# Strided attention on one core: another order of the first loads, stores of two groups at once, and transposes ahead of the sums

## The chip, the cores and the metric

The kernel runs on one core of a Trainium2 chip. The metric is the device time of one execution in microseconds (us), lower is better. Executions of the kernel before agree within about 0.3%. A profiled execution shows the span of the core, which is some 1.8 to 2.1 us shorter than the device time.

## The reference

```python
Q, K, V: float32 [8, 12, 1024, 64]; stride = 64
attend_positions = np.arange(0, seq, stride)           # 16 keys per head
scores  = einsum('bhqd,bhkd->bhqk', q, k) / sqrt(64)
weights = softmax(scores)                              # over the 16 keys
result  = einsum('bhqk,bhkd->bhqd', weights, v)        # float32
```

Every query of the 96 heads attends to 16 keys. The arithmetic is small. 25.2 MB of Q must be read and 25.2 MB of result written, and only 0.79 MB of K and V is used, in rows of 256 bytes.

## The kernel before

Four heads make a group: 1 MiB of Q, 1 MiB of output, 24 groups. All DMAs are issued by SyncE (SP) on one queue, in program order. An issue that has to wait holds up every issue behind it: in the profiled run the transposes of group 0 ended, and freed a load buffer, at 16.2 us, but SyncE issued nothing between 14.61 us and the first store at 25.18 us, and the next load behind that store at 25.91 us.

```python
QBUFS = 11                      # Q groups in flight
OBUFS = 9                       # output groups in flight
nc.sync.dma_start(k_raw, _ap_with(K, kv_src))      # 1,536 rows of 256 bytes
nc.sync.dma_start(v_raw, _ap_with(V, kv_src))      # the same
for g in range(QBUFS):
    load(g)                     # 32 rows of 32 KiB
# ... k_dup, k_t from K; v_bf (GpSimd cast), v_bd from V:
for n in range(2):
    for c in range(2):
        vp = psum_sc.tile(...)
        nc.tensor.matmul(vp, lhsT=perm_v..., rhs=v_bf...)     # waits for V
        for s in range(4):
            nc.vector.tensor_scalar(out=v_bd..., in0=vp, ...)
# ... then the main part
for g in range(2):
    for x in range(2):
        transposes(g, x)        # TensorE, then a ScalarE copy to qt
scores(0)                       # TensorE, then exp on ScalarE to w
for g in range(NG):
    sums(g)                     # TensorE, reciprocal on VectorE
    outputs(g, 0)               # TensorE, multiply on VectorE to out_sb
    outputs(g, 1)
    if g + 1 < NG:
        scores(g + 1)
    outputs(g, 2)
    if g + 2 < NG:
        transposes(g + 2, 0)
    outputs(g, 3)
    if g + 2 < NG:
        transposes(g + 2, 1)
    store(g)                    # 128 rows of 8 KiB from SBUF
    if g + QBUFS < NG:
        load(g + QBUFS)
```

TensorE works in program order too: the last of the four `vp` matmuls, which stand ahead of the first transposes, started at 14.02 us and the transposes at 14.29. So a late V holds up everything (in the changed kernel the transposes started at 18.89 us, and at 10.93 us with V's work moved behind them: after_v_later).

The softmax here doesn't subtract the row's maximum and nothing guards it: scores larger than these inputs give would overflow.

## Time and profile before

| | before |
|---|---|
| device time | 130.33 us (130.28 to 130.64) |
| span of the profiled run | 128.5 us |
| DMA queue, share of 16 engines | 96.3% |
| ScalarE, VectorE, TensorE busy | 67%, 65%, 54% |
| compute ends, last DMA packet ends | 114.2 us, 127.1 us |

The page's second part shows the span in 40 slices of 3.2 us; in the DMA row, 9 is 90% busy or more. The third part gives the queues' packets, bytes and share. From both, before the change:

```profile
DMA  2999989999899899999999999999998999999980
GB/s 57 351 398 418 449 367 490 388 423 439 339 421 487 357 441 439 413 434 449 383 467 426 393 459 428 393 469 421 405 469 357 416 434 416 421 428 421 434 337 23
...
q1 hardware_dynamic: 7712, 51.12, 96.3%
```

The DMA engines are full from the second slice to the end. The chain of waits of the same page says otherwise at first sight:

```profile
ACT 60%; PE 13%; DVE 5%; DMA 3%; POOL 3%; issue 2%; ACTq 1%; DVEq 0%; POOLq 0%
```

That chain is followed back from the last compute. The waits of SyncE's own queue show that this compute is not the end: the kernel's last wait (L307) is for stores that had been issued long before.

```profile
SPq L307 <- DMA out_dram<-out_sb: 12.6, 1, 12.6
```

Columns: in all, times, longest, in us. So a faster ScalarE gains nothing here (loop_only, below, took 12 us of waiting from its exp: ratio 0.999). What counts is whether the DMA engines always have work. For that, SyncE's timeline (start, length, instruction):

```profile
0.73 0.44 SPq L89 DMA_DIRECT2D k_raw<-in_K_dram  x1
1.23 0.71 SPq L90 DMA_DIRECT2D v_raw<-in_V_dram  x1
1.99 12.62 SPq L34 DMA_DIRECT2D qn<-in_Q_dram  x11
25.18 0.63 SPq L34 DMA_DIRECT2D out_dram<-out_sb  x1
25.91 0.55 SPq L34 DMA_DIRECT2D qn<-in_Q_dram  x1
28.33 0.59 SPq L34 DMA_DIRECT2D out_dram<-out_sb  x1
```

The first store is issued at 25.18 us. In the trace's packet records (start, duration and size of each DMA packet) its data start at 33.35 us on average, because eleven loads stand ahead of it. And this is how V reaches the first transposes:

```profile
7.80 0.83 POOL L124 CAST v_bf<-v_raw 128x768 bf16<-128x768 f32 x1
...
9.68 8.49 DVE L180 TENSOR_SCALAR v_bd<-vp,mask 128x384 bf16<-128x384 f32 x16
...
14.29 1.91 PE L193 MATMUL qt_ps<-identity,qn 128*128 128x128 bf16 x16
```

### The profile page before, as it was taken

To read this page: it belongs to the slowest core of one execution; us is meant where nothing else is said; L and a number is where in the kernel's file an instruction comes from. 1 tells how busy PE (TensorE), PEld (TensorE's weight loads), DVE (VectorE), ACT (ScalarE), POOL (GpSimd) and SP (SyncE) were. 2 spreads that over 40 slices of the span, in tenths; PEclk is the share of its full clock that TensorE was granted. 3 is DMA by queue.
4 is the path that set the end of the run, shared out by engine and by line. 5 is a ranking of instruction groups with operands and counts; after the bars stand their busy time and mean duration, and the time that the engine had idled before them with its cause. 6 is when DMAs were issued, how large, how long until landed. Compare 5 with 4: busy or idle time off the path is not lost.

```text
span 128.5 us, 2215 instructions
## 1 busy us (share of the span) xinstructions
PE 69.4 (54%) x880; PEld 51.1 (40%) x880; DVE 83.7 (65%) x144; ACT 86.3 (67%) x103; POOL 5.1 (4%) x23
## 2 busy tenths in 40 slices
PE   0071665975656866558766578665687655510000
PEld 0040542754445654445544456443465444300000
DVE  6229963787677777787777877877877778750000
ACT  2163294988889888898888898888988888400000
POOL 4470000000000000000000000000000000000000
PEclk9999997799999999999999999999999999955555
DMA  2999989999899899999999999999998999999980
GB/s 57 351 398 418 449 367 490 388 423 439 339 421 487 357 441 439 413 434 449 383 467 426 393 459 428 393 469 421 405 469 357 416 434 416 421 428 421 434 337 23
DMA packets 7722, 51.26 MB, mean 399 GB/s; under 512 B 3872, under 2 KB 3872, under 8 KB 3872
## 3 DMA queue, kind: packets, MB, share of 16 engines
q1 hardware_dynamic: 7712, 51.12, 96.3%
q8 instruction: 7, 0.11, 0.4%
q14 instruction: 3, 0.02, 0.0%
HBM read 25.95 MB, written 25.17 MB: 398 GB/s over the span
## 4 chain that ended last, share of the span: by engine, by line
ACT 60%; PE 13%; DVE 5%; DMA 3%; POOL 3%; issue 2%; ACTq 1%; DVEq 0%; POOLq 0%
ACT qt L198 34%; ACT w L218 26%; PE sc L206 8%; DVE v_bd L180 3%; DMA k_raw<-in_K_dram 3%; PE qt_ps L193 2%; PE o_ps L238 2%; DVE out_sb L243 1%; POOL k_dup L116 1%; POOL perm_v L120 1%; PE sm L227 1%; POOL v_bf L124 1%; ACTq L307 1%; DVEq L307 0%; PE vp L175 0%
## 5 line engine op out<-in xcount | busy, mean ns | idle before, releaser
L243 DVE TENSOR_TENSOR out_sb<-o_ps,rec 128x512 f32<-128x512 f32 x96 | 63.3, 688 | 15.3 <-PE o_ps L238 12.9
L198 ACT COPY qt<-qt_ps 128x1024 bf16<-128x1024 bf16 x48 | 46.2, 1015 | 5.2 <-PE qt_ps L193 4.7
L218 ACT ACTIVATE w<-sc 64x512 bf16<-64x512 f32 x48 | 35.4, 737 | 13.2 <-PE sc L206 12.9
L238 PE MATMUL o_ps<-v_bd,w 128*128 128x256 bf16 x192 | 33.4, 278 | 0.6 <-DVE out_sb L243 0.6
L193 PE MATMUL qt_ps<-identity,qn 128*128 128x128 bf16 x384 | 30.7, 227 | 0.2 <-ACT qt L198 0.2
L193 PEld LDWEIGHTS <-qn 128*128 128x128 bf16 x384 | 27.0, 102 | 3.9 <-issue 2.6
L206 PE MATMUL sc<-qt,k_t 128*32 128x512 bf16 x96 | 9.8, 395 | 24.5 <-ACT qt L198 24.5
L238 PEld LDWEIGHTS <-w 128*128 128x128 bf16 x192 | 14.3, 98 | 6.9 <-issue 6.2
L206 PEld LDWEIGHTS <-k_t 128*32 128x32 bf16 x96 | 4.4, 93 | 29.3 <-issue 29.2
L231 DVE RECIPROCAL rec<-sm 128x32 f32<-128x32 f32 x24 | 8.6, 358 | 9.0 <-PE sm L227 9.0
L227 PE MATMUL sm<-s_sel,w 128*128 128x4 bf16 x192 | 8.5, 166 | 6.9 <-ACT w L218 6.9
L227 PEld LDWEIGHTS <-w 128*128 128x128 bf16 x192 | 6.4, 96 | 11.0 <-ACT w L218 11.0
L180 DVE TENSOR_SCALAR v_bd<-vp,mask 128x384 bf16<-128x384 f32 x16 | 8.5, 608 | 0.1
L166 ACT CAST k_t<-kp 64x512 bf16<-64x512 f32 x6 | 3.5, 579 | 3.6 <-PE kp L160 3.5
L160 PE MATMUL kp<-perm_k,k_dup 128*128 128x128 bf16 x12 | 1.5, 312 | 6.7 <-POOL k_dup L116 6.7
L175 PE MATMUL vp<-v_bf,perm_v 128*128 128x384 bf16 x4 | 1.8, 490 | 4.6 <-DVE v_bd L180 4.1
L160 PEld LDWEIGHTS <-k_dup 128*128 128x128 bf16 x12 | 1.2, 145 | 6.7 <-POOL k_dup L116 6.7
L138 DVE TENSOR_SCALAR slot_i<-iota_p 128x1 int16<-128x1 int16 x1 | 0.2, 156 | 4.7 <-POOL iota_p L136 4.7
L166 ACT ACT_TABLE_LOAD x1 | 1.3, 1283 | 2.5 <-DVE k_t L127 2.5
L127 DVE MEMSET k_t<- 128x1536 uint32 x1 | 1.3, 1338 | 1.1 <-PEq L293 1.1
L175 PEld LDWEIGHTS <-perm_v 128*128 128x128 bf16 x4 | 0.5, 127 | 3.7 <-issue 3.7
L116 POOL CAST k_dup<-k_raw 128x768 bf16<-128x768 f32 x2 | 1.6, 827 | 3.0 <-DMA k_raw<-in_K_dram 3.0
(15 smaller groups left out, 6.0 us busy)
## 6 DMA issues: line engine op xcount, KB each, us to landing
qn<-in_Q_dram SPq DMA_DIRECT2D x24, 1024.0 KB, 19.0
out_dram<-out_sb SPq DMA_DIRECT2D x24, 1024.0 KB, 19.5
k_raw<-in_K_dram SPq DMA_DIRECT2D x1, 384.0 KB, 4.3
v_raw<-in_V_dram SPq DMA_DIRECT2D x1, 384.0 KB, 5.4
```

The source lines that it names most:

```text
L116: nc.gpsimd.tensor_copy(out=k_dup[:, :, e], in_=k_raw)
L160: nc.tensor.matmul(kp[:, i], lhsT=k_dup[:, 4 * n + i].rearrange("p e d -> p (e d)"), rhs=pk, start=True, stop=True,)
L166: nc.scalar.copy(k_t[h, 4 * n : 4 * n + 4, :, :, e].rearrange("p n c s k -> p (n c s) k"), kp[h].rearrange("p n c s k -> p (n c s) k"),)
L180: nc.vector.tensor_scalar(out=v_bd[:, 6 * n : 6 * n + 6, c, s], in0=vp, scalar1=mask[:, s : s + 1], scalar2=None, op0=ALU.mult,)
L193: nc.tensor.transpose(ps[:, i], _ap_with(qb, [qb.ap[0], [2, P]], extra_offset=(8 * x + i) * 2 * P + 1), identity,)
L198: nc.scalar.copy(qt[g][:, x], ps)
L206: nc.tensor.matmul(sc[32 * j : 32 * j + 32], lhsT=kt[:, 32 * j : 32 * j + 32], rhs=_ap_with(q, [q.ap[0], [P, 8], [8 * P, 2], [1, 32]], ext ...
L218: nc.scalar.activation(out=_ap_with(wa, [wa.ap[0], [P, 8], [1, 2], [2, 32]], extra_offset=64 * a), in_=sc[64 * a : 64 * a + 64].rearrange( ...
L227: nc.tensor.matmul(sm[:, :, i], lhsT=wt[g][:, i], rhs=s_sel, start=True, stop=True)
L231: nc.vector.reciprocal(rec[g], sm.rearrange("p b i e -> p b (i e)"))
L238: nc.tensor.matmul(ps[:, :, i], lhsT=wt[g][:, 2 * c + i], rhs=v_bd[:, g // 2, g % 2].rearrange("p s d -> p (s d)"), start=True, stop=True,)
L243: nc.vector.tensor_tensor(out=out_sb[g][:, :, 4 * c : 4 * c + 4], in0=ps.rearrange("p b i (e d) -> p b (i e) d", e=2), in1=rec[g][:, :, 4 ...
```

## The change

The intent: start with the large Q packets instead of K's small ones, make store packets twice as large, and take ScalarE's wait for the scores out of the loop. Buffers are redistributed: 10 loads, and 5 stores of double size.

```diff
-    QBUFS = 11
-    OBUFS = 9
+    QBUFS = 10
+    OBUFS = 5
-    nc.sync.dma_start(k_raw, _ap_with(K, kv_src))
-    nc.sync.dma_start(v_raw, _ap_with(V, kv_src))
     for g in range(QBUFS):
         load(g)
+        if g == 0:
+            nc.sync.dma_start(k_raw, _ap_with(K, kv_src))
+        elif g == 1:
+            nc.sync.dma_start(v_raw, _ap_with(V, kv_src))
 ...  (out_sb holds two groups; its index becomes [:, g % 2, :, ...])
-            _ap_with(out, [[16 * D, P], [2 * SD, 2], [1, 16 * D]], g * HG * SD),
-            _ap_with(o, [o.ap[0], [1, 1], [1, 32 * D]]),
+            _ap_with(out, [[16 * D, P], [2 * SD, 4], [1, 16 * D]], n * 2 * HG * SD),
+            _ap_with(o, [o.ap[0], [1, 1], [1, 64 * D]]),
 ...
     for g in range(NG):
+        if g + 2 < NG:
+            transposes(g + 2, 0)
         sums(g)
         outputs(g, 0)
-        outputs(g, 1)
         if g + 1 < NG:
             scores(g + 1)
-        outputs(g, 2)
-        if g + 2 < NG:
-            transposes(g + 2, 0)
-        outputs(g, 3)
+        outputs(g, 1)
         if g + 2 < NG:
             transposes(g + 2, 1)
-        store(g)
-        if g + QBUFS < NG:
-            load(g + QBUFS)
+        outputs(g, 2)
+        outputs(g, 3)
+        if g % 2 == 1:
+            store(g // 2)
+            for n in (g - 1, g):
+                if n + QBUFS < NG:
+                    load(n + QBUFS)
```

More of the change, by code (lines that the diff above doesn't have):

```diff
@@ L233, in outputs @@
     def outputs(g, c):
-        if c == 0:
-            out_sb[g] = out_pool.tile([P, 2, 16, D], FP32, name="out_sb", tag="out_sb")
+        if c == 0 and g % 2 == 0:
+            out_sb[g // 2] = out_pool.tile(
+                [P, 2, 2, 16, D], FP32, name="out_sb", tag="out_sb"
+            )
         ps = psum_o.tile([P, 2, 2, 2 * D], FP32, name="o_ps", tag="o")
@@ L243, in outputs @@
         nc.vector.tensor_tensor(
-            out=out_sb[g][:, :, 4 * c : 4 * c + 4],
+            out=out_sb[g // 2][:, g % 2, :, 4 * c : 4 * c + 4],
             in0=ps.rearrange("p b i (e d) -> p b (i e) d", e=2),
@@ L248, in outputs, with store @@
         )
-    def store(g):
-        o = out_sb[g]
+    def store(n):
+        o = out_sb[n]
         _copy(
             nc,
-            _ap_with(out, [[16 * D, P], [2 * SD, 2], [1, 16 * D]], g * HG * SD),
-            _ap_with(o, [o.ap[0], [1, 1], [1, 32 * D]]),
+            _ap_with(out, [[16 * D, P], [2 * SD, 4], [1, 16 * D]], n * 2 * HG * SD),
+            _ap_with(o, [o.ap[0], [1, 1], [1, 64 * D]]),
         )
```

## The prediction

> **What bounds it now.** The DMA engines. The DMA queue table gives the kernel's queue 96.3% of 16 engines' span (51.1 MB in 128.5 us); the 40-slice rows show DMA at 8 to 9 tenths from slice 2 to the end, while VectorE and ScalarE are at 65% and 67% (busy table). The chain of waits names ScalarE (60%), but compute ends at 114.2 us (timeline) and SyncE then waits 12.6 us for the last store (waits of the DMA queue). [...] in the trace's packet records an 8 KiB store packet takes 312 ns and a 32 KiB load packet 1,239 ns, times 16 engines 420 and 423 GB/s. So only DMA time without full work can be won: about 2.3 us before the first packet, a 1 us ramp while K's 256-byte packets start, some 2.3 us of skew at the end (engines run dry between about 124.3 and 127.6 us), and 0.9 us after.
>
> **What the change does.**
>
> 1. Store packets grow from 8 to 16 KiB. Comparing (4 x 312 - 1,239)/3, a packet costs 3 ns extra; 1,536 fewer over 16 engines is 0.3 us. Twelve fewer DMAs save semaphore writes: 0.1 us.
> 2. Q block 0 first: K's slow ramp hides behind it: about 0.5 us.
> 3. K lands at about 6.6 instead of 5.0 us; V behind two Q blocks (2.49 us each) and K at about 10.8 instead of 6.6 us. V is waited for: today its cast on GpSimd starts at 7.86, the v_bd masks run from 9.68, and TensorE, in program order, starts the first transposes at 14.3, after the last vp matmul. This chain moves about 3 us later.
> 4. The first store now needs groups 0 and 1. Today SyncE issues stores at 25.18 and 28.33 us, while 11 Q loads keep the engines busy until the first store packets at about 33.5 us: 7 us of slack. Afterwards 10 loads end at about 30.8 us. Laying the new program order over the durations in the timeline, group 1 ends at about 28.8 in the old time base, plus 3: the store is issued at about 31.9, its first bytes move 1.4 us later (as K's do after their issue). The loads of groups 10 and 11 stand behind that store in SyncE's order. So the DMA engines run dry for about 2.5 us.
> 5. The new order removes ScalarE's 0.5 us wait for scores in each group: its period falls from 3.94 to about 3.45 us (busy 0.97 x 2 + 0.74 x 2). This is off the critical path: the DMA needs 4.9 us for a group. Five double buffers hold ten groups, so no new store wait is expected.
>
> **Sum.** Span 128.5 - 0.4 - 0.5 + 2.5 - 0.1 (skew) is about 130.0; the run time is 1.8 us above the span: **131.8 us** (range 130.0 to 133.1). Chance of faster by over 2%: 0.03; within 2%: 0.82; slower by over 2%: 0.15.
>
> **What would show it.** Right: a dip in the DMA row near 31 to 34 us; SyncE's first store issue near 32; the first transposes near 17.3; the first load packet near 2.3 us; store packets of 16 KiB near 620 ns; the scores' wait gone and groups every 3.45 us; compute still ending well before the last store. Wrong: no dip, or a first store before 29 us.
>
> **What would make it wrong.** V landing earlier than 10.8, or group 1 ending sooner: then there is no gap and about 129.3 remains. A larger share of small-packet time hidden behind Q. Different skew at the end. A slower 16 KiB store (its four 4 KiB pieces lie 512 KiB apart), which would cost each 1% of store time about 0.6 us.

## The result, and the profile after

The changed kernel takes 134.3 us (134.17 to 135.12, six runs; the two near 135.1 had the lowest mean TensorE clock, 0.86), the kernel before in the same rounds 130.51 us. The ratio is 1.031 (95% interval 1.028 to 1.034). Ratios here are the mean time of one kernel's fast runs over that of the other's of the same rounds, so not quite the ratio of the medians quoted. The change loses 3%.

The same parts of the page, after the change:

```profile
DMA  6799989994998999999999999999999899999980
GB/s 159 236 381 414 426 377 466 416 387 183 446 317 317 389 466 411 374 466 416 401 451 411 401 461 431 382 441 456 387 416 471 372 431 436 411 426 431 431 372 35
...
q1 hardware_dynamic: 5984, 51.12, 95.2%
```

The tenth slice (29.8 to 33.1 us) has fallen to 4 tenths and 183 GB/s: the dip. Two slices further on (36.4 to 43.0 us) there is something else: the busy share is back at 8 and 9, but the engines move only 317 GB/s. They are busy with packets that take too long. (The page counts a packet, its time and its bytes, in the slice in which it starts, so single slices are rough.)

The chain of waits is now headed by DMA, because in the second half compute waits for Q:

```profile
DMA 42%; ACT 22%; DVE 9%; PE 8%; issue 4%; POOL 2%; POOLq 1%; DVEq 1%; SPq 0%; ACTq 0%
```

The waits of SyncE's queue end as before: stores are still draining for 13.2 us after the last issue.

```profile
SPq L313 <- DMA out_dram<-out_sb: 13.2, 3, 4.9
```

SyncE's timeline after the change:

```profile
0.74 0.59 SPq L34 DMA_DIRECT2D qn<-in_Q_dram  x1
1.38 0.56 SPq L101 DMA_DIRECT2D k_raw<-in_K_dram  x1
1.99 0.96 SPq L34 DMA_DIRECT2D qn<-in_Q_dram  x1
2.99 0.59 SPq L103 DMA_DIRECT2D v_raw<-in_V_dram  x1
3.63 9.22 SPq L34 DMA_DIRECT2D qn<-in_Q_dram  x8
31.74 0.64 SPq L34 DMA_DIRECT2D out_dram<-out_sb  x1
32.48 1.90 SPq L34 DMA_DIRECT2D qn<-in_Q_dram  x2
38.39 0.59 SPq L34 DMA_DIRECT2D out_dram<-out_sb  x1
```

SyncE issues nothing between 12.85 and 31.74 us. The loads of groups 10 and 11 could have gone long before (the transposes of groups 0 and 1 are done by 23 us), but they stand behind the store. And V's way to the first transposes:

```profile
12.39 0.83 POOL L126 CAST v_bf<-v_raw 128x768 bf16<-128x768 f32 x1 [1.52 <-DMA v_raw<-in_V_dram]
...
14.28 8.49 DVE L182 TENSOR_SCALAR v_bd<-vp,mask 128x384 bf16<-128x384 f32 x16
...
18.89 1.91 PE L195 MATMUL qt_ps<-identity,qn 128*128 128x128 bf16 x16
```

The cast now waits for V (in brackets: idle before, and releaser), and the first transposes come 4.6 us later.

The packet records allow an exact account. Following the packets of each engine from end to start gives 16 chains; this table has their averages. (Another way of chaining moves single groups by about 1%, the sums not at all.) SyncE's first issue is set to 0.735 us in every run. (The prediction had placed the packets about 0.5 us later on the same clock.)

| us, mean of 16 engines | before | after | difference |
|---|---|---|---|
| up to the first Q packet, K and V included wherever they stand | 5.69 | 5.36 | -0.33 |
| in load packets (48 per engine) | 59.46 | 61.54 | +2.08 |
| in store packets | 59.95 | 60.21 | +0.26 |
| dip before the first store (before: the longest gap there) | 0.18 | 1.72 | +1.54 |
| other gaps and overlaps | -0.32 | 0.30 | +0.62 |
| from the mean end to the last engine's end | 2.13 | 1.75 | -0.38 |
| from there to the end of the span | 1.42 | 1.36 | -0.06 |
| span | 128.50 | 132.24 | +3.74 |

The load packets are slow in two places above all. The first three Q groups take 1,654, 1,289 and 1,369 ns a packet instead of 1,405, 1,224 and 1,227. Groups 10 and 11, the first loads after the dip, take 1,398 and 1,514 instead of 1,274 and 1,218. In between, groups 3 to 9 are alike within 2%; the groups after 11 add some 0.3 us in all. The first store of 2 MiB takes 707 ns a packet, later ones 616 in the median. Two packets of 8 KiB took 622 before.

Two details of the packet records matter later. The first store is not slow from its start: the first six packets of an engine take 615 to 641 ns on average, the last two 772 and 1,153, and the loads right behind them are slow too. And the first Q group's packets must be read together with their start: in other kernels with this load order they start up to 0.5 us later and take 1,390 to 1,520 ns, and the group ends at 5.4 to 5.6 us in all of them.

### The profile page after: what moved, and what is told of

Read it like the earlier page. It is cut to its first block, busy times and chain, and to the rows that moved or that the text cites. A ratio compares the mean times of both kernels' runs of the same rounds, so it can differ in the third digit from the quotient of the medians.

```text
span 132.2 us, 2191 instructions
## 1 busy us (share of the span) xinstructions
PE 73.8 (56%) x880; PEld 53.9 (41%) x880; DVE 82.4 (62%) x144; ACT 84.9 (64%) x103; POOL 5.1 (4%) x23
## 4 chain that ended last, share of the span: by engine, by line
DMA 42%; ACT 22%; DVE 9%; PE 8%; issue 4%; POOL 2%; POOLq 1%; DVEq 1%; SPq 0%; ACTq 0%
DMA qn<-in_Q_dram 37%; ACT qt L200 13%; ACT w L220 8%; DMA k_raw<-in_K_dram 5%; DVE out_sb L247 5%; PE qt_ps L195 4%; DVE v_bd L182 3%; PE o_ps L242 2%; POOL k_dup L118 1%; PE sc L208 1%; POOL perm_v L122 1%; POOLq L313 1%; PE sm L229 1%; DVE rec L233 0%; DVEq L313 0%
## 5 line engine op out<-in xcount | busy, mean ns | idle before, releaser
L247 DVE TENSOR_TENSOR out_sb<-o_ps,rec 128x512 f32<-128x512 f32 x96 | 62.6, 688 | 7.8 <-PE o_ps L242 5.3
L200 ACT COPY qt<-qt_ps 128x1024 bf16<-128x1024 bf16 x48 | 47.1, 1014 | 18.9 <-PE qt_ps L195 18.4
L195 PE MATMUL qt_ps<-identity,qn 128*128 128x128 bf16 x384 | 34.2, 242 | 14.5 <-DMA qn<-in_Q_dram 14.2
L195 PEld LDWEIGHTS <-qn 128*128 128x128 bf16 x384 | 29.4, 110 | 20.2 <-DMA qn<-in_Q_dram 15.6
L242 PE MATMUL o_ps<-v_bd,w 128*128 128x256 bf16 x192 | 35.5, 292 | 0.7 <-DVE out_sb L247 0.7
L242 PEld LDWEIGHTS <-w 128*128 128x128 bf16 x192 | 15.1, 102 | 7.6 <-issue 6.5
L229 PEld LDWEIGHTS <-w 128*128 128x128 bf16 x192 | 7.0, 98 | 7.8 <-ACT w L220 7.7
L208 PEld LDWEIGHTS <-k_t 128*32 128x32 bf16 x96 | 3.7, 94 | 11.3 <-issue 11.3
```

The source lines that it names most:

```text
L195: nc.tensor.transpose(ps[:, i], _ap_with(qb, [qb.ap[0], [2, P]], extra_offset=(8 * x + i) * 2 * P + 1), identity,)
L200: nc.scalar.copy(qt[g][:, x], ps)
L208: nc.tensor.matmul(sc[32 * j : 32 * j + 32], lhsT=kt[:, 32 * j : 32 * j + 32], rhs=_ap_with(q, [q.ap[0], [P, 8], [8 * P, 2], [1, 32]], ext ...
L229: nc.tensor.matmul(sm[:, :, i], lhsT=wt[g][:, i], rhs=s_sel, start=True, stop=True)
L242: nc.tensor.matmul(ps[:, :, i], lhsT=wt[g][:, 2 * c + i], rhs=v_bd[:, g // 2, g % 2].rearrange("p s d -> p (s d)"), start=True, stop=True,)
L247: nc.vector.tensor_tensor(out=out_sb[g // 2][:, g % 2, :, 4 * c : 4 * c + 4], in0=ps.rearrange("p b i (e d) -> p b (i e) d", e=2), in1=rec ...
```

## The experiments

Theory A: the queue runs dry before the first store (late V, two groups instead of one, one load less, and the next loads behind the store), and this costs the dip and slow packets after it. Rivals: the 16 KiB stores are slow in themselves (B); the load order costs by itself (C). Later: why packets are slow around the first store (D to G).

This table gathers what matters from all runs. "Lead" is the time from the first store's issue to its first data, averaged over the engines: the queue's reserve. "Dip" is the longest gap of that stretch, averaged over the engines; 0.1 to 0.2 us is usual where no dip is seen. "Loads" and "stores" are the sums of packet time per engine.

| kernel | us | ratio | first store issued | lead | dip | loads | stores |
|---|---|---|---|---|---|---|---|
| before | 130.4 | 1 | 25.18 | 8.2 | 0.18 | 59.46 | 59.95 |
| loop_only | 130.29 | 0.999 | 24.63 | 8.8 | 0.15 | 59.50 | 59.93 |
| kv_early | 129.81 | 0.996 | 27.92 | 7.9 | 0.14 | 59.68 | 59.46 |
| order_only | 131.15 | 1.006 | 29.83 | 4.0 | 0.15 | 60.32 | 60.00 |
| after_early_loads | 130.46 | 1.000 | 32.77 | 3.7 | 0.09 | 60.30 | 59.52 |
| after_kv_first | 130.24 | 1.001 | 28.12 | 2.7 | 0.11 | 60.21 | 59.62 |
| pair_only | 130.57 | 1.002 | 28.49 | 2.3 | 0.16 | 60.30 | 59.70 |
| after_single | 131.56 | 1.009 | 29.14 | 2.2 | 0.18 | 60.78 | 60.35 |
| after_q11 | 132.13 | 1.014 | 32.80 | 1.5 | 0.38 | 60.88 | 60.12 |
| after_v_later | 132.74 | 1.017 | 30.47 | 1.4 | 0.51 | 61.21 | 60.14 |
| after | 134.3 | 1.031 | 31.74 | 1.35 | 1.72 | 61.54 | 60.21 |
| before_q7 | 134.72 | 1.034 | 24.57 | 1.3 | 2.59 | 60.19 | 60.59 |
| before_q6 | 137.17 | 1.051 | 25.12 | 1.35 | 5.65 | 60.20 | 60.70 |

In the three runs with the largest dips the lead was 1.3 to 1.35 us: that is what an issue into an empty queue needed here before data moved.

The column "first store issued" holds one accident. Most runs, the kernel before among them, show a stretch of about 3.5 us before or around the first store in which TensorE's granted clock was near 0.5 (0.50 from 20.8 to 24.2 us in the kernel before). The profiled runs of pair_only, after_v_later, after_pitch and of the kernel after the change show none there. With the same compute up to the first store, it was issued at 31.74 us without such a stretch (after) and at 32.77 to 32.84 us with one (after_early_loads, after_q11, after_stagger). So up to 1.1 us of this column, and of the lead, can come from the clock. It does not explain the loss, since the profiled run after the change had none.

### order_only

The kernel before with the new load order alone.

```diff
-    nc.sync.dma_start(k_raw, ...)
-    nc.sync.dma_start(v_raw, ...)
     for g in range(QBUFS):
         load(g)
+        if g == 0: nc.sync.dma_start(k_raw, ...)
+        elif g == 1: nc.sync.dma_start(v_raw, ...)
```

> The kernel before with nothing but the new load order (Q block 0, K, Q block 1, V). Theory A (the change loses time because the queue runs dry before the first store and the engines restart slowly): the first store moves from 25.2 to about 29.7 us, eleven Q loads end near 34.3 us, so no dip; only the first Q packets are slow as after the change (about +0.8 us, less 0.3 us of ramp saved): 130.8 to 131.2 us. Rival C (the order itself costs the time): 132.5 us or more, with no dip in the DMA row.

Measured: 131.15 us (130.84 to 131.28), ratio 1.006 (1.004 to 1.007). First store at 29.83 us, no dip. The first Q group took 1,651 ns a packet, as after the change; load time +0.86 us, start -0.37 us. Theory A's numbers hold. The order costs 0.6% by itself, not 3%.

### pair_only

The kernel before with paired stores, 10 load and 5 store buffers; loads and loop order are those of before.

```diff
-    QBUFS = 11
-    OBUFS = 9
+    QBUFS = 10
+    OBUFS = 5
 ...  out_sb and store(n) as in the change
-        store(g)
-        if g + QBUFS < NG:
-            load(g + QBUFS)
+        if g % 2 == 1:
+            store(g // 2)
+            for n in (g - 1, g):
+                if n + QBUFS < NG:
+                    load(n + QBUFS)
```

> The kernel before with stores of two groups, 10 load buffers and 5 store buffers, K and V first, the old loop order. Theory A: first store issued near 28.3 us, ten loads end near 30.8 us, so the queue is only just fed: no dip or one under 0.3 us, store packets of 16 KiB near 617 ns from the start, 129.9 to 130.7 us. Rival B (the store of 16 KiB rows is slow in itself at its start): packets of 800 to 1,200 ns in the first two stores and loads of 1,400 to 1,500 ns around them also without a dip, 131.5 us or more.

Measured: 130.57 us (130.38 to 131.04), ratio 1.002 (1.000 to 1.004). The time is A's and there is no dip. But group 11 took 1,586 ns a packet and the first store 664: a part of B's sign, without a dip. So slow packets don't need a dip. The lead here is 2.3 us. The expected 617 ns from the start is missed.

### after_kv_first

The changed kernel with K and V in front again.

```diff
+    nc.sync.dma_start(k_raw, ...)
+    nc.sync.dma_start(v_raw, ...)
     for g in range(QBUFS):
         load(g)
-        if g == 0: nc.sync.dma_start(k_raw, ...)
-        elif g == 1: nc.sync.dma_start(v_raw, ...)
```

> The changed kernel with K and V first again. Theory A: first store issued near 27.2 us, before the ten loads end at 30.8 us: no dip, no slow packets after it, 129.8 to 130.5 us, so the whole loss of 3.8 us is gone. Rival B (store shape): slow packets around the first stores remain, 131.5 us or more.

Measured: 130.24 us (130.00 to 130.92), ratio 1.001 (0.998 to 1.004): the whole loss is gone. "No slow packets" was wrong (group 11: 1,527 ns, lead 2.7 us). Their cost is made up by faster stores (59.62 instead of 59.95 us) and by less skew at the end (1.00 instead of 2.13 us).

### after_early_loads

The changed kernel, new load order included, with the loads ahead of the store they need not wait for.

```diff
+        if g + QBUFS < NG:
+            load(g + QBUFS)
         if g % 2 == 1:
             store(g // 2)
-            for n in (g - 1, g):
-                if n + QBUFS < NG:
-                    load(n + QBUFS)
```

> The changed kernel, but load(g + 10) issued at the end of each loop turn, ahead of the pair's store instead of behind it; the new load order is kept. Theory A: loads of groups 10 and 11 are queued before 25 us and keep the engines busy past 36 us: no dip, no slow packets after it, only the slow first Q packets remain, 130.4 to 131.2 us. Rival B (store shape) or C (order): 132.5 us or more.

Measured: 130.46 us (130.09 to 130.60), ratio 1.000 (0.999 to 1.002). The first store was issued even later than after the change (32.77 us), with the same V and the same pairing, and it did not matter. The DMA row and the rates of its page:

```profile
DMA  4799898998989989989999989989989999999981
GB/s 153 250 374 424 346 478 366 458 458 351 478 346 463 427 364 468 443 364 453 422 407 438 443 382 463 433 377 438 473 382 402 443 443 407 407 443 448 407 351 46
```

There is no slice of 4 in the tenth place, and no pair of slices near 317 GB/s. Groups 10 to 13 took 1,242 to 1,254 ns. This is the plainest proof of A: two lines moved, no data changed, 3.8 us back.

### before_q7 and before_q6

The opposite test: make the old kernel's queue run dry, with its 8 KiB stores, its order, K and V first.

```diff
-    QBUFS = 11
+    QBUFS = 7        # and 6
```

> The kernel before with 7 load buffers instead of 11 and nothing else: seven Q loads end near 23.6 us, the first store is still issued near 25.2 us and its first bytes move 1.8 us later, as after the change. Theory A (a dry queue costs its length, plus slow packets after the restart): a dip of about 3.3 us in the DMA row near 24 to 27 us, slow packets in the 12 us after it worth 0.5 to 1.7 us, together 133.8 to 135.5 us. Rival B (the slow packets belong to the 16 KiB stores alone): the dip alone, packets at their usual 311 and 1,219 ns, 133.3 to 133.8 us. If dips cost nothing: 130.5 us.

> The kernel before with 6 load buffers: the queue runs dry another 2.5 us earlier than with 7 (there a gap of 2.6 us and 134.7 us). Theory A: the gap grows to about 5.1 us and the slow packets after the restart cost the same 1.4 us or so: 136.8 to 137.8 us. If slow packets grew with the gap: above 138 us.

Measured: 134.72 us (134.45 to 134.95) with 7, ratio 1.034 (1.032 to 1.035); 137.17 us (136.92 to 137.22) with 6, ratio 1.051 (1.049 to 1.053). The dip was 2.59 and 5.65 us. The extra packet time over before stayed the same: loads +0.73 and +0.74, stores +0.64 and +0.75. So here a dry queue cost its length once, and about 1.4 us besides. Not all of that needs a dry queue: in pair_only the loads took 0.84 us longer without a dip. Both times lie in the expected ranges; the dips had been put at 3.3 and 5.1 us. Rival B falls: 8 KiB stores show it too. With 7 buffers:

```profile
DMA  2998997298989998999998998999999999999980
GB/s 65 330 465 356 445 465 326 101 378 252 529 363 398 492 410 376 494 393 388 477 435 361 465 437 378 452 435 386 447 437 400 437 440 403 418 423 423 425 336 22
```

The eighth slice is the dip (2 tenths, 101 GB/s). The tenth is the slow stretch: 8 tenths busy, but only 252 GB/s. In the packet records, all 16 engines start the first store between 25.85 and 26.00 us. The first five packets of an engine take 309 to 328 ns on average, the last three 436, 533 and 639, and the load behind takes 1,726 ns a packet.

### after_q11

More reserve by another way: the changed kernel with one load buffer more, one store buffer less.

```diff
-    QBUFS = 10
-    OBUFS = 5
+    QBUFS = 11
+    OBUFS = 4
```

> The changed kernel with 11 load buffers and 4 double store buffers (about the same memory): the eleventh Q load keeps the engines busy 2.5 us longer, to about 34.3 us, and the first store's bytes come at 33.5 us. Theory A: no dip, 130.4 to 131.5 us, the new load order and pairing notwithstanding. Rival: if order and pairing cost time in another way, 133 us or more.

Measured: 132.13 us (132.04 to 132.14), ratio 1.014 (1.012 to 1.015). More than half of the loss is gone, but the expectation is missed by 0.6 us. The store was issued 1.1 us later than after the change (32.80 instead of 31.74), so the lead was 1.5 us, not comfortable, and a gap of 0.38 us was left. V was not the reason: the first transposes started at 18.95 us, against 18.89. TensorE's granted clock was, in this profiled run: 0.55 from 26 to 28 us and 0.59 from 28 to 30, where it was 1.00 after the change. In the clock rows (the change above, this run below) it is the 5 in the ninth slice:

```profile
PEclk9999999999999999999999869869959959995555
PEclk9999999959999999999999999955959968965555
```

The slow packets came too (first store 704 ns, group 12 1,513 ns).

### after_v_later

The changed kernel, with V's work moved behind the first transposes.

```diff
-    for n in range(2):
+    def v_half(n):
         for c in range(2):
 ...
             transposes(g, x)
+        if g == 0:
+            v_half(0)
     scores(0)
+    v_half(1)
```

> The changed kernel with the v_bd work moved: its first half between the transposes of groups 0 and 1, its second after the scores of group 0, so that V, which now lands at 12 us, no longer holds up the first transposes. Loads, stores and their order are as changed. Theory A (V's late landing, through TensorE's program order, is what makes the first store late): first transposes near 11 us instead of 18.9, outputs from about 22.8 us when v_bd is ready, first store near 28.5 us, before the queue runs dry at 31.4: no dip, 130.5 to 131.5 us. If something else sets the first store: no change, 134 us.

Measured: 132.74 us (132.39 to 133.16), ratio 1.017 (1.015 to 1.020). The first transposes did come at 10.93 us. But the first store came only 1.3 us sooner (30.47 us), not 3.2, because the second half of V's matmuls was held up until 19.35 us: it waits for the exp, whose input holds one of the two PSUM buffers.

```profile
19.35 0.80 PE L178 MATMUL vp<-v_bf,perm_v 128*128 128x384 bf16 x2 [1.92 <-ACT w L221]
```

The expectation is missed, the direction is right: 1.3 us earlier, 1.2 us less dip, 1.6 us less time. V's late landing is one link of the chain to the first store, and shortening that chain gains.

### after_single

The changed kernel with stores of one group (and one load behind each).

```diff
-    OBUFS = 5
+    OBUFS = 10
 ...  out_sb and store(g) as in the kernel before
-        if g % 2 == 1:
-            store(g // 2)
-            for n in (g - 1, g):
-                if n + QBUFS < NG:
-                    load(n + QBUFS)
+        store(g)
+        if g + QBUFS < NG:
+            load(g + QBUFS)
```

> The changed kernel with stores of one group (10 store buffers) and loads as in the kernel before, one behind each store; load order, load buffers and loop order stay changed. Theory A: the first store needs group 0 alone and is issued near 28.9 us, before the queue runs dry at 31.4 us: no dip, 130.7 to 131.6 us, about that of the load order alone (131.15). If pairing has no part in it: 134 us.

Measured: 131.56 us (131.03 to 132.24), ratio 1.009 (1.005 to 1.013). No dip; first store at 29.14 us. So pairing is a necessary link too. Group 10 was slow (1,666 ns a packet) at a lead of 2.2 us.

### loop_only

The kernel before with the new order of the loop alone (the `if` lines are left out of this cut).

```diff
+            transposes(g + 2, 0)      # now first in the turn
         sums(g)
         outputs(g, 0)
-        outputs(g, 1)
         scores(g + 1)
-        outputs(g, 2)
-        transposes(g + 2, 0)
-        outputs(g, 3)
+        outputs(g, 1)
         transposes(g + 2, 1)
+        outputs(g, 2)
+        outputs(g, 3)
```

> The kernel before with nothing but the new order of the loop (transposes ahead of the sums, scores after the first output). All theories: ScalarE's period falls from 3.94 to about 3.35 us a group, but the DMA engines set the time: 130.1 to 130.8 us.

Measured: 130.29 us (130.20 to 130.42), ratio 0.999 (0.997 to 1.001). The profile's group of the exp (busy and mean ns, then idle before) shows that the wait is gone:

```profile
L218 ACT ACTIVATE w<-sc 64x512 bf16<-64x512 f32 x48 | 35.4, 738 | 1.2 <-PE sc L206 0.5
```

Before, this group had 13.2 us of idle time. Twelve microseconds of waiting were taken from ScalarE's exp, and nothing was gained: in the same run the idle time of ScalarE's copies (L198) rose from 5.2 to 14.3 us, waiting for transposes that wait for Q.

### kv_early

K and V first, the other parts of the change, and the loads ahead of the store (after_kv_first and after_early_loads together).

```diff
+    nc.sync.dma_start(k_raw, ...)
+    nc.sync.dma_start(v_raw, ...)
     for g in range(QBUFS):
         load(g)
-        if g == 0: nc.sync.dma_start(k_raw, ...)
-        elif g == 1: nc.sync.dma_start(v_raw, ...)
 ...
+        if g + QBUFS < NG:
+            load(g + QBUFS)
         if g % 2 == 1:
             store(g // 2)
-            for n in (g - 1, g):
-                if n + QBUFS < NG:
-                    load(n + QBUFS)
```

> The changed kernel with K and V first and with the loads ahead of the store: the candidate for the best of both. Theory A: no dip, fewer slow packets than with K and V first alone (there the load of group 11 took 1,527 ns a packet), 129.4 to 130.2 us. If the time is simply the DMA floor, it can't be told from before: within 0.4% of it.

Measured: 129.81 us (129.69 to 129.97), ratio 0.996 (0.9945 to 0.9975). It beats the kernel before by 0.4% and the changed one by 3%. Its store packets take 0.49 us less per engine than before, with a lead of 7.9 us. That is all the idea was worth.

### after_pitch

Why are packets slow where the engines start together? One guess (theory D) was that they read memory at the same spacing. The packet records hold no addresses, so the spacing of the engines in it is the author's estimate. This kernel is wrong in three groups.

```diff
-    _ap_with(Q, [[HG * SD // 32, 32], [1, HG * SD // 32]], g * HG * SD)
+    _ap_with(Q, [[HG * SD // 32 + (512 if g in (0, 10, 11) else 0), 32],
+                 [1, HG * SD // 32]], g * HG * SD)
```

> The changed kernel with the source rows of the loads of groups 0, 10 and 11 spaced 34 KiB instead of 32 KiB (wrong data for these groups on purpose; the same bytes and packets). It asks why the load packets are slow where all 16 engines start together. Theory D (the engines read at a 64 KiB spacing in lockstep and get in each other's way in the memory): first Q packets fall from 1,655 to about 1,300 ns, those of groups 10 and 11 from 1,398 and 1,514 to about 1,230, 132.5 to 133.2 us. Rival E (a common restart is slow whatever the addresses): no change, 134.1 to 134.6 us. The dip of about 1.7 us stays in both.

Measured: 134.31 us (133.75 to 135.21), ratio 1.031 (1.026 to 1.036). Groups 0, 10 and 11 took 1,516, 1,321 and 1,593 ns. The rows lie 32 KiB apart; they went to 34 KiB and the slow packets stayed. Groups 10 and 11 together took as long as before the padding (2,914 and 2,912 ns), and group 0's 1,516 ns is what kernels with this order show without padding too (1,513 in after_q11). Theory D falls in this form.

### after_stagger

The last try at that cause: put the engines out of step by cutting the first store.

```diff
+        for p0, p1 in ([(0, 8), (8, 16), (16, 128)] if n == 0 else [(0, 128)]):
+            r = o[p0:p1]
+            _copy(nc, _ap_with(out, [[16 * D, p1 - p0], ...], ... + p0 * 16 * D), ...)
```

> The changed kernel with the first store cut into three: partitions 0 to 7, 8 to 15 and 16 to 127, so that eight of the DMA engines should get two rows of 16 KiB more than the other eight (9 against 7) and the two halves run 1.2 us out of step after the dip. Theory F (engines in step hinder each other): the slow packets after the dip shrink by a half or more: first store's mean from 707 to below 660 ns, loads of groups 10 and 11 from 1,398 and 1,514 to below 1,350 ns. Rival G (a restart from an empty queue is slow by itself): means as before. The time says little here, since the uneven share itself may cost up to 0.6 us: 133 to 135 us.

Measured: 139.06 us (two runs, 138.65 and 139.46), ratio 1.067, outside the expected 133 to 135. It is inconclusive. The three issues took 3.16 us of SyncE's time, the longest gap of an engine grew to 4.3 us on average, and the first packets took 2.2 to 2.5 us each with half of the engines idle. What made these packets so slow was not shown. So the run tested its own hindrance, and why packets are slow there stays open.

## Why the prediction was right or wrong

The prediction said 131.8 us and most likely no difference beyond 2%. The kernel took 134.3 us, outside its range.

- **What bounds it: right.** loop_only took the exp's waits from ScalarE and gained nothing, while every kernel with a dip lost time. The DMA engines drain the queue in order here: in the packet records of the kernel before, the first store's data come 8.2 us after its issue, behind the loads. That the packets themselves could not be much faster than 420 and 423 GB/s over 16 engines was the author's estimate; in the steady state a packet gained 1% here (next point).
- **Larger store packets: right, and small.** 616 instead of 622 ns for 16 KiB is 0.58 us over 96 packets per engine (predicted 0.3). Twelve fewer DMAs are also 192 fewer packets of 4 bytes, 16 per DMA (800 before, 608 after, 9 ns each on average): the 0.1 us that the prediction puts down to semaphore writes. The larger packets show as -0.43 us of store time in after_early_loads and -0.49 in kv_early, where little else disturbs it. After the change it was eaten by the slow first store.
- **Q first saves the ramp: right in size** (-0.33, predicted -0.5 us), but Q's first group then pays more than this: +0.25 us a packet, two packets an engine. Up to the end of the third group the new order costs about 0.6 us net. order_only shows the order as a loss of 0.6%.
- **V lands late and moves the first transposes: right in mechanism, short in size.** The first transposes came 4.6 us later, not 3. The first Q group, ahead of K and V, took 1.65 instead of 1.24 us a packet, which accounts for 0.8 us of the missing 1.6; the rest was not traced.
- **The first store: right by luck, errors that cancel.** 31.74 us, predicted 31.9. The start was 1.6 us later than thought. Against that, with K and V first the changed kernel issued it at 28.12 us, not the 28.8 laid out (after_kv_first), and that run had the slow clock (0.50 from 22 to 24 us), which the profiled run after the change did not: 28.12 plus 4.6 is 32.7 us, as measured where the clock was slow (32.77 to 32.84).
- **The dip: right in place and cause, smaller in size.** 1.7 us, predicted 2.5. Undoing the load order, the pairing, or the loads' place behind the store each took it away (after_kv_first, after_single, after_early_loads), and starving the old kernel brought it about (before_q7).
- **The step that failed is the sum**, "128.5 - 0.4 - 0.5 + 2.5 - 0.1". It charged for the dip alone and took every packet's duration from the steady state. The term of packet time, -0.3 in the prediction, measured +2.34 us: +2.08 for loads and +0.26 for stores; other gaps came to +0.62. About 0.9 us of the loads' share lies in the first three groups and 0.8 in the two groups after the dip. before_q7 and before_q6 show that such a cost goes with a dry queue whatever its length (1.4 us of packet time at dips of 2.6 and 5.7 us).
- **What stays open** is why those packets are slow. It goes with a short lead: where K and V come first, the load packets sum to 59.5 to 59.7 us at leads of 7.9 us and more, and to 60.2 to 60.3 at leads of 2.7 us and less, with or without a dip. "Slow after a restart" is not quite it: the first store begins at the usual rate, and the slow packets are its last ones and the loads behind it, in before_q7 as after the change. The spacing of the rows, 34 instead of 32 KiB, did not matter (after_pitch: 2,914 instead of 2,912 ns for groups 10 and 11 together). That the engines run in step is only argued.

## What to carry to other kernels

Where the DMA engines are the limit, look for the moment at which the queue is nearest to empty, here between the first burst of loads and the first store, and count the reserve there (8.2 us before, 1.35 us after). Making a store larger (pair_only, with one load less: 2.3 us left), a constant later (order_only: 4.0) or the burst shorter (before_q7: 1.3, and dry) all drew on the same reserve. Don't issue a load behind a store that it need not wait for: here it inherited the store's wait, and going ahead of the store gave 3.8 us back (after_early_loads). Charge a dry queue with more than its length (here about 1.4 us more, at dips of 2.6 and 5.7 us), and don't take packet times of the steady state for the start (1,654 instead of about 1,220 ns a load packet after the change) and for the first store and the loads behind it (707 instead of 616 ns, and up to 1,514 instead of 1,218).

## What these runs measured of the DMA queue

- From an issue to its first data it took 0.7 us from the end of the issue and 1.35 us from its start, for a store of 2 MiB into an empty queue (after), and 1.1 us from its start for K (before).
- A queue that ran dry cost more than the dry time: about 1.4 us of longer packets in the 10 us that follow (in the last packets of the first store and the load behind it, not at once), at dips of 2.6 and 5.7 us alike (before_q7, before_q6), and as much load time at a lead of 2.3 us without a dip (group 11 in pair_only: 1,586 instead of 1,218 ns a packet).
- With rows 32 KiB apart, 2 KiB more per row did not cure the slow packets (groups 10 and 11: 1,321 and 1,593 ns with the padding in after_pitch, 1,398 and 1,514 without in the kernel after).
- K and V leave gaps of 3.14 us in an engine's chain of Q packets after the change, for 192 packets of 256 bytes: 16.4 ns each. At the rate of a 32 KiB packet (1,219 ns) 256 bytes would take 9.5 ns. So, as an estimate from these two, some 42% of the time is overhead of all kinds, if the gaps hold nothing else.
